# Six small changes in a two-layer hybrid decoder kernel: first products, one weight subtraction, the output projection's split, the index queries, the last selection rounds and the pins of late weights

## The chip, the cores and the metric

The kernel runs on one core of one Trainium2 chip. The metric is device time in microseconds (us), the median of several executions. The engines of the core are TensorE (PE: matrix products and transposes), VectorE (DVE: element-wise work and reductions), ScalarE (ACT: exponentials, casts, copies), GpSimd (POOL: some casts, subtractions and copies) and SyncE (SP), which issues most of the DMAs. Each engine runs its own list of instructions in the order of the program and waits on semaphores for the others.

## The reference

A sequence of 512 positions of width 1024 goes through two decoder layers, batch 1, all in float32. Layer 0 mixes by multi-head latent attention (MLA), layer 1 by a sparse attention (DSA). Each layer then attends with 4 heads to 256 memory tokens and ends with a gated feed-forward network. After every sub-layer comes `x <- LayerNorm(alpha * x + sublayer(x))`.

```
mla:  h = x @ w_in;  q = rms_norm(h[:, :512]) @ w_uq;  k, v = rms_norm(h[:, 512:768]) @ w_ukv  (+ rotary key, 32 wide)
      out = causal softmax(q k^T * 96^-0.5) v @ w_o                          # 16 heads, nope 64 + rope 32, v 64
dsa:  h = x @ w_in -> q (16 heads x 64), k, v (4 groups x 64), q_idx (8 x 64), k_idx (64), w_idx (8)
      index score = sum over 8 heads of  w_idx * relu(q_idx . k_idx / 8),  causal
      each query keeps its top 128 keys;  softmax(q k^T / 8 + rel_bias) v over those keys, then @ w_o
```

## The kernel before

The 512 positions are 4 query tiles of 128. A float32 factor is split into a high part (ACT casts it) and a low part (DVE or POOL subtracts the high part from the original, line L106), and each product is three matmuls: high by high, high by low, low by high (L137, L138, L139). Weights come by `chunk`: a DMA on SP into one of three `raw` buffers, a cast `wh` on ACT (L104), a subtraction `wl` on DVE or POOL (L106). `behind(ins)` asks that an instruction be put, on its own engine's list, after a given earlier point; the framework's scheduler then fixes the order of each list from its own estimates. So the order on an engine is not simply that of the source text.

**The start.** Eight small matmuls on an identity (`WARM`, L145) run before the data is there. Then the first projection of MLA takes the eight column blocks of `x` in order; for each block and tile it issues the three products together.

**The MLA middle.** The query part of the first projection is normalised tile by tile in `rms_t`: ACT sums the squares (L612), DVE and POOL make the reciprocal root (L298 on DVE, L300 on POOL), DVE scales (L615), PE transposes (L618), and ACT and DVE split the result. Two weights wait to be split there: `w_uk`, whose low part is a DVE instruction (L106 `wl<-raw,wh`, 128x1024) held behind the scaling of the last tile (`rms_scaled`), and the first of `w_uq`, whose low parts are POOL's. A raw buffer goes back to SP for the next weight when the low part of the old one has been made.

**The end of MLA.** `out_proj_parts` is a generator: it issues the products of the first piece `c == 0` of the output projection for the first half of the columns (24 matmuls), yields, and goes on after the last head's value products (`mla_pv(15)`).

**The DSA stage.** In the trace it lies between about 755 and 940 us. In order: the value and index-key projections; per pair of index heads `j` (0 to 3) a query projection, 12 score matmuls (L1130, L1131), 6 relus on ACT (L1133) and 6 accumulations on DVE (L1135, L1137); two key projections; eight query projections (`j` = 0 to 7); then attention over 16 items. An item is a query tile `qt` and a key group `g`, so item 4 is the first of tile 1 (keys 256 wide), item 8 the first of tile 2 (384 wide), item 12 the first of tile 3 (512 wide). Its steps are `s` (scores: PE L1205, L1206, L1207; bias add and minimum on DVE L498; exponential on ACT L505), `t` (transposes: PE L1220, split on ACT L104 and DVE L106) and `p` (values: PE L1251, L1252, L1262; ACT L1254; DVE L1259, L1263). Steps of the first items are run between the query projections (`steps`).

The top 128 keys of a query are found on DVE in 16 rounds for each of the tiles 1 to 3, 48 in all. A round is a maximum of 8 (L1149 `MAX8`) and a replacement of these 8 (L1150 `MATCH_REPLACE8`), 256, 384 or 512 wide. The rounds of a tile form one chain over one buffer. `NTK` says how many rounds stand in the source before each query projection, `NTI` how many after each later item; the scheduler may bring a round forward on DVE's list. When a tile's 16 rounds are done, ACT turns the buffer into a mask (L1156, `make_mask`), and PE adds that mask to the scores of that tile by a matmul (L1205).

**Queues around the output projection of DSA.** SP's list holds, in order, the reads of the relative bias for each item (L1186, `reads`), loads of the output weights `dsa_o` (L118) and reloads of the residual (L167). `pins` hold a weight load behind a certain bias read, and the POOL subtraction of the first weights behind a step of an item.

## Time and profile before

| | us |
|---|---|
| median of 3 executions (1501.17 to 1501.28) | 1501.27 |
| the profiled execution | 1501.13 |
| its span (first to last instruction) | 1499.3 |
| PE busy in the span | 1475.3 (98%) |
| DVE busy | 1041.7 (69%) |
| ACT busy | 672.8 (45%) |
| POOL busy | 401.6 (27%) |
| mean granted PE clock | 0.998 |

The span is the time from the first to the last instruction that the profile shows; 1.8 us of the profiled execution lie around it. A row of the timeline gives start, duration, engine, line, operation and the tiles by the program's names, then, in brackets, how long the engine had stood idle before it and what ended that. Rows of windows give for each engine its busy time and the count of instructions in a stretch, then the granted PE clock, the DMA share and the GB/s. Rows of groups give the count, the busy time and the mean duration of one. Line numbers in this document are those of the kernel before, unless a row of the order of the changed kernel is shown: there, lines from L582 on are 5 to 16 higher.

### The profile page before, as it was taken

The numbers are of one execution on the slowest core, as the hardware profiler recorded it, in microseconds if no ns is written. First come the engines' busy times: TensorE is split into PE (matmuls) and PEld (weight loads), VectorE is DVE, ScalarE is ACT, GpSimd is POOL, SyncE is SP. The second block draws the span as 40 slices with busy tenths as digits, with TensorE's granted clock in tenths as the row PEclk, the third lists the DMA queues.
The fourth block names the chain that finished last, engine by engine and source line by source line (L and its number), as shares of the span: only waits on it lengthen the run. The fifth ranks groups of instructions, "written<-read, shape, count | busy, mean of one in ns | idle before, by whom it ended". The sixth has DMA issues, their size and how long they took to land. (4 is left out here: it accounts for less than half of the span.)

```text
span 1499.3 us, 20324 instructions
## 1 busy us (share of the span) xinstructions
PE 1475.3 (98%) x7600; PEld 1258.1 (84%) x7600; DVE 1041.7 (69%) x1792; ACT 672.8 (45%) x1198; POOL 401.6 (27%) x368
## 2 busy tenths in 40 slices
PE   9999999999999999999999989999999999999998
PEld 8788888988888888888898768898889888888886
DVE  7766769667847656565778989685687575566656
ACT  4777743455233333333256688244542333334321
POOL 1454403010125223240025652030102233152302
PEclk9999999999999999999999999999999999999999
DMA  6244424423233332233333246353242333223231
GB/s 221 71 106 108 168 85 142 139 71 127 74 105 100 120 99 97 96 99 114 105 127 94 68 149 225 113 169 99 71 141 71 99 101 124 97 91 121 71 98 57
DMA packets 50282, 166.17 MB, mean 111 GB/s; under 512 B 5189, under 2 KB 11605, under 8 KB 47365
## 3 DMA queue, kind: packets, MB, share of 16 engines
q1 hardware_dynamic: 49460, 163.35, 33.6%
q10 hardware_dynamic: 720, 1.51, 0.3%
q8 instruction: 60, 0.98, 0.3%
q14 instruction: 42, 0.34, 0.1%
HBM read 160.60 MB, written 9.47 MB: 113 GB/s over the span
## 5 line engine op out<-in xcount | busy, mean ns | idle before, releaser
L137 PE MATMUL ps<-t,wh 128*128 128x512 f32 (+2 forms) x1184 | 433.3, 366 | 0.4 <-DVE t L106 0.3
L139 PE MATMUL ps<-t,wl 128*128 128x512 f32 (+2 forms) x1184 | 432.0, 365 | 1.4 <-DVE wl L106 1.4
L138 PE MATMUL ps<-t,wh 128*128 128x512 f32 (+2 forms) x1184 | 432.1, 365 | 0.0
L104 ACT CAST wh<-raw 128x1024 fp32r<-128x1024 f32 (+1 forms) x199 | 207.7, 1044 | 312.2 <-PE ps L138 136.5
L106 DVE TENSOR_TENSOR wl<-raw,wh 128x1024 fp32r<-128x1024 f32 (+2 forms) x170 | 234.8, 1384 | 108.9 <-ACT wh L104 108.0
L137 PE MATMUL ps<-wh,t 128*128 128x512 f32 (+2 forms) x736 | 281.7, 383 | 0.0
L138 PE MATMUL ps<-wl,t 128*128 128x512 f32 (+2 forms) x736 | 279.9, 380 | 0.1
L139 PE MATMUL ps<-wh,t 128*128 128x512 f32 (+2 forms) x736 | 279.5, 380 | 0.0
L139 PEld LDWEIGHTS ps<-t,wl 128*128 128x128 f32 x1184 | 223.3, 189 | 36.8 <-DVE wl L106 1.7
L137 PEld LDWEIGHTS ps<-t,wh 128*128 128x128 f32 x1184 | 223.3, 189 | 36.6 <-DVE t L106 1.6
L138 PEld LDWEIGHTS ps<-t,wh 128*128 128x128 f32 x1184 | 223.4, 189 | 34.5
L104 ACT CAST t<-ps 128x512 fp32r<-128x512 f32 (+3 forms) x241 | 118.2, 524 | 134.9 <-PE ps L368 85.9
L104 ACT CAST wh<-t 128x1024 fp32r<-128x1024 f32 (+1 forms) x84 | 82.3, 980 | 199.4 <-PE ps L138 163.8
L106 DVE TENSOR_TENSOR t<-ps,t 128x512 fp32r<-128x512 f32 (+3 forms) x241 | 137.8, 604 | 32.6 <-ACT t L104 31.4
L139 PEld LDWEIGHTS ps<-wh,t 128*128 128x128 f32 x736 | 138.5, 188 | 25.5
L137 PEld LDWEIGHTS ps<-wh,t 128*128 128x128 f32 x736 | 138.7, 188 | 24.9 <-ACT t L104 0.2
L138 PEld LDWEIGHTS ps<-wl,t 128*128 128x128 f32 x736 | 138.6, 188 | 24.9 <-DVE wl L106 0.5
L106 DVE TENSOR_TENSOR wl<-t,wh 128x1024 fp32r<-128x1024 f32 (+1 forms) x84 | 101.4, 1208 | 77.8 <-ACT wh L104 76.3
L300 POOL TENSOR_TENSOR sm<-sm,mhalf 128x1 f32<-128x1 f32 x32 | 28.3, 883 | 435.9 <-DVE sm L298 435.9
L104 ACT CAST t<-t 128x512 fp32r<-128x512 f32 (+3 forms) x133 | 75.4, 573 | 84.1 <-POOL t L944 51.6
L1015 DVE TENSOR_TENSOR t<-ps,t 128x512 f32<-128x512 f32 x44 | 30.4, 692 | 115.4 <-PE ps L139 115.4
L106 DVE TENSOR_TENSOR t<-t,t 128x512 fp32r<-128x512 f32 (+3 forms) x112 | 86.1, 775 | 33.1 <-ACT t L104 30.4
(184 smaller groups left out, 1924.8 us busy)
## 6 DMA issues: line engine op xcount, KB each, us to landing
raw<-in_ffn_in_dram SPq DMA_DIRECT2D x88, 512.0 KB, 3.5
t<-in_ffn_dg_dram SPq DMA_DIRECT2D x16, 1024.0 KB, 5.1
raw<-in_xa_k_dram SPq DMA_DIRECT2D x16, 512.0 KB, 3.6
raw<-in_xa_v_dram SPq DMA_DIRECT2D x16, 512.0 KB, 4.1
raw<-in_xa_q_dram SPq DMA_DIRECT2D x16, 512.0 KB, 3.6
scr<-vscr SPq DMA_DIRECT2D x16, 319.5 KB, 4.2
raw<-in_w_uq_dram SPq DMA_DIRECT2D x8, 512.0 KB, 3.9
raw<-in_mla_o_dram SPq DMA_DIRECT2D x8, 512.0 KB, 5.5
```

The costliest lines, as they stand in the source:

```text
L104: high[0] = nc.scalar.copy(h, src)
L106: low[0] = (eng or nc.vector).tensor_tensor(l, src, h.bitcast(F32), op=ALU.subtract)
L137: nc.tensor.matmul(ps, st[0], mv[0], start=start, stop=False, skip_group_check=more)
L138: nc.tensor.matmul(ps, st[0], mv[1], start=False, stop=False, skip_group_check=more)
L139: return nc.tensor.matmul(ps, st[1], mv[0], start=False, stop=stop, skip_group_check=more)
L300: power[0] = nc.gpsimd.tensor_tensor(b, a, mhalf, op=ALU.pow)
L1015: nc.vector.tensor_tensor(sg, pu, sg, op=ALU.mult)
```

## The change

- `WARM` is 9 instead of 8, and for the first column block the four tiles' high-by-high products come first, then the four high-by-low, then the four low-by-high.
- `rms_scaled` is taken before the five calls of `mla_v` and the last `rms_t`, so the low part of `w_uk` is held behind the scaling of the third tile, not of the fourth.
- `out_proj_parts` yields after piece `c == 1`, so 48 matmuls instead of 24 stand before the last head's value products. (The generator serves all output projections; only this call stops at the yield for other work.)
- The index queries of pair `j + 1` are projected before the scores of pair `j`.
- `NTK` ends with 2 instead of 4. Two rounds follow the last query projection and its steps, their maxima held behind `reduced[0]`, the latest bias add (L498) at that point, which is that of item 5. All later rounds of that tile chain behind them. The masks of tiles 2 and 3 are asked for one item earlier.
- The pins of `dsa_o` weights 3 to 7 are reads 10, 11, 12, 13, 14 in place of 6, 8, 10, 12, 14.

```
-WARM = 8
+WARM = 9
...
-                    if c == 0:
+                    if c == 1:
                         norm = yield
...
+            if k == 0:
+                for n, (x_, w_) in enumerate(((xh, wh), (xh, wl), (xl, wh))):
+                    for tt in range(NT):
+                        nc.tensor.matmul(ps2[tt][:, 0:NC0], x_[:, ts_of(tt)], w_, start=n == 0, stop=False)
+                continue
...
+    rms_scaled = scaled[0]
     for hv in range(5):
         mla_v(hv)
     rms_t(psq[NT - 1], 512, NT - 1, gq, cq)
     rms_end = high[0], low[0]
-    rms_power, rms_scaled = power[0], scaled[0]
+    rms_power = power[0]
...
+    waiting = index_queries(0)
+    for j in range(4):
+        ahead_q = index_queries(j + 1) if j < 3 else None
+        index_scores(j, waiting)
+        waiting = ahead_q
...
-    NTK, NTI = (5, 5, 5, 5, 5, 4, 4, 4), 2
+    NTK, NTI = (5, 5, 5, 5, 5, 4, 4, 2), 2
...
+    for _ in range(2):
+        topk(*todo.pop(0), reduced[0])
...
-        if n in (4, 8):
-            make_mask(2 + n // 8, outs[-1])
+        if n in (3, 7):
+            make_mask(2 + n // 7, outs[-1])
 
-    pins = [(reads[max(4, 2 * c)] if c > 2 else None, spreads[1 + 2 * c] if c < 5 else None) for c in range(NK)]
+    pins = [(reads[7 + c] if c > 2 else None, spreads[1 + 2 * c] if c < 5 else None) for c in range(NK)]
```

How the lists change is shown at three places. The first is DVE in the MLA middle (`wl` is the low part of `w_uk`, `t_113` the scaled last tile). Before:

```order
L298 TENSOR_SCALAR sm_596<-sm_594 128x1
L615 SCALAR_TENSOR_TENSOR t_113_600<-ps_485,sm_598,t_35_278 128x512
L106 TENSOR_TENSOR t_12_124<-ps_519,t_12_124 128x2x128
L106 TENSOR_TENSOR t_14_126<-ps_533,t_13_125 128x4x128
L106 TENSOR_TENSOR t_102_546<-ps_547,t_102_546 128x4x64
L106 TENSOR_TENSOR t_102_546<-ps_556,t_102_546 128x4x64
L106 TENSOR_TENSOR t_102_546<-ps_565,t_102_546 128x4x64
L106 TENSOR_TENSOR wl_632<-raw_629,wh_631 128x1024
```

and of the change:

```order
L298 TENSOR_SCALAR sm_597<-sm_595 128x1
L106 TENSOR_TENSOR wl_633<-raw_630,wh_632 128x1024
L106 TENSOR_TENSOR t_12_125<-ps_520,t_12_125 128x2x128
L106 TENSOR_TENSOR t_14_127<-ps_534,t_13_126 128x4x128
L106 TENSOR_TENSOR t_102_547<-ps_548,t_102_547 128x4x64
L106 TENSOR_TENSOR t_102_547<-ps_557,t_102_547 128x4x64
L106 TENSOR_TENSOR t_102_547<-ps_566,t_102_547 128x4x64
L620 SCALAR_TENSOR_TENSOR t_113_601<-ps_486,sm_599,t_35_279 128x512
```

The big subtraction moved from behind four or five low parts to the place right after the last tile's L298, and the scaling of the last tile moved behind those low parts.

The second place is ACT just after that (`t_13` from `ps_602` or `ps_603` is the high part of the last normalised tile, which the first query products read; `wh_929` or `wh_930` is the cast of the second `w_uq` weight, used by later heads). Before:

```order
L104 CAST t_13_125<-ps_602 128x4x128
L675 CAST t_115_609<-t_84_480 64x512
L676 CAST t_115_609<-t_84_480 64x512
L104 CAST t_115_609<-ps_635 64x512
L104 CAST wh_929<-raw_927 128x1024
```

and of the change:

```order
L104 CAST wh_930<-raw_928 128x1024
L104 CAST t_13_126<-ps_603 128x4x128
L681 CAST t_115_610<-t_84_481 64x512
L682 CAST t_115_610<-t_84_481 64x512
L104 CAST t_115_610<-ps_636 64x512 x2
```

The cast of the second `w_uq` weight now stands ahead of the cast that the first query products wait for. Likewise POOL's subtraction of that weight now stands ahead of its casts L681 and L682.

The third place is DVE around item 5's scores in the DSA stage (`t_1758` and `t_1756` are item 5, `t_1503` is the index score buffer of tile 3). Before, ahead of and at item 5:

```order
L1149 MAX m_1801_11774<-t_1503_10574 128x8
L1150 MATCH_REPLACE t_1503_10574<-m_1801_11774,t_1503_10574 128x512
L1149 MAX m_1802_11777<-t_1503_10574 128x8
L509 RECIPROCAL sm_11593<-sm_11500 128x4
L1150 MATCH_REPLACE t_1503_10574<-m_1802_11777,t_1503_10574 128x512
L1149 MAX m_1823_11848<-t_1503_10574 128x8
L1150 MATCH_REPLACE t_1503_10574<-m_1823_11848,t_1503_10574 128x512
L1149 MAX m_1824_11851<-t_1503_10574 128x8
L1259 TENSOR_TENSOR t_1748_11585<-ps_11580,t_1747_11583 64x256 x2
L498 ISA t_1758_11618,sm_11620<-ps_11622,t_1758_11618 128x256
```

and of the change, at and behind item 5:

```order
L498 ISA t_1756_11613,sm_11615<-ps_11635,t_1756_11613 128x256
L498 ISA sm_11615 128x1
L1165 MAX m_1763_11641<-t_1503_10575 128x8
L498 ISA t_1627_11135,sm_11647<-ps_11649,t_1627_11135 128x128
L498 ISA sm_11647 128x1
L106 TENSOR_TENSOR t_1752_11601<-ps_11595,t_1751_11600 128x512
L1166 MATCH_REPLACE t_1503_10575<-m_1763_11641,t_1503_10575 128x512
L106 TENSOR_TENSOR t_1755_11610<-ps_11604,t_1754_11609 128x512
L1165 MAX m_1764_11644<-t_1503_10575 128x8
L498 ISA t_1627_11135,sm_11647<-ps_11654,t_1627_11135 128x128
```

Before, the maxima of 15 of tile 3's 16 rounds stand ahead of item 5's first L498 and one round and a half stand between it and the first L498 of item 8. With the change 7 rounds stand ahead of it and 9 between item 5's last and item 8's first L498, each split by other work; nothing of tile 3's selection is left after item 8 begins in either.

## The prediction

> **What bounds the kernel now.** I read the page first: PE is busy for nearly the whole span, so time can be won only where PE stands still, and is lost wherever PE must wait anew.

> ```profile
> span 1499.3 us, 20324 instructions
> PE 1475.3 (98%) x7600; PEld 1258.1 (84%) x7600; DVE 1041.7 (69%) x1792; ACT 672.8 (45%) x1198; POOL 401.6 (27%) x368
> ```

> That leaves 24.0 us of PE idle time. The waits of PE say where it lies: of what the change touches, one wait in the MLA middle, and in the DSA stage (800 to 905 us) these:

> ```profile
> PE ps L1206 <- DVE sm L498: 2.6, 1, 2.6
> PE ps L1220 <- DVE t L1259: 1.3, 1, 1.3
> PE ps L1205 <- ACT t L1156: 0.7, 2, 0.5
> ```

> Columns are the total, the times and the longest. The timeline shows the first of these from both sides: PE finishes item 5's scores by 864.5, but the next score bank comes free only when DVE has done item 5's first L498, and that is queued behind selection rounds.

> ```profile
> 863.17 0.28 PE L1207 MATMUL ps<-t,t 128*128 128x256 f32 x1
> 864.23 0.28 PE L1207 MATMUL ps<-t,t 128*128 128x256 f32 x1
> 867.15 0.39 PE L1206 MATMUL ps<-t,t 128*128 128x256 f32 x1 [2.64 <-DVE sm L498]
> ...
> 863.67 0.69 DVE L1149 MAX8 m<-t 128x8 f32<-128x512 f32 x1
> 865.19 0.69 DVE L1149 MAX8 m<-t 128x8 f32<-128x512 f32 x1
> 866.66 0.42 DVE L498 CUSTOM_DVE_ANT_0 t<-ps,t 128x256 f32<-128x256 f32 x1
> 884.93 0.55 DVE L498 CUSTOM_DVE_ANT_0 t<-ps,t 128x384 f32<-128x384 f32 x1
> ```

> The last row is item 8's first L498. The windows (engine busy times in the order PE, PE loads, DVE, ACT, POOL) show a PE-bound stretch with a DVE that is nearly full, one where both wait for each other, and a rest where both have about 3 us free:

> ```profile
> 849.00:863.40 14.40, 14.40 (x80) 12.38 (x79) 14.01 (x43) 9.67 (x26) 8.53 (x13) 1.00 0.26 84
> 863.40:884.90 21.50, 16.83 (x100) 14.17 (x99) 18.29 (x63) 15.94 (x47) 12.41 (x20) 0.92 0.34 116
> 884.90:905.00 20.10, 17.20 (x101) 14.36 (x101) 16.96 (x54) 17.72 (x46) 11.25 (x22) 1.00 0.57 202
> ```

> The same windows for the two instructions of a round, L1149 and then L1150 (DVE busy, count):

> ```profile
> 849.00:863.40 14.40, 4.86 (x7) 1.00 0.26 84
> 863.40:884.90 21.50, 2.08 (x3) 0.92 0.34 116
> ```

> ```profile
> 849.00:863.40 14.40, 5.04 (x14) 1.00 0.26 84
> 863.40:884.90 21.50, 2.46 (x7) 0.92 0.34 116
> ```

> A 512-wide round costs (4.86 + 5.04) / 7 = 1.41 us of DVE. In the first window PE has no gap: there DVE does 9.9 us of rounds beside PE's query projections, for nothing.

> **The selection rounds, part by part.** The order shows that all rounds behind the 39th now come after item 5's last L498: the two held maxima carry the whole chain of tile 3 with them. So 9 rounds stand between item 5 and item 8, where 4.54 us of rounds lay.

> First, the wait removed. Item 5's first score is ready at 863.17 + 0.28 = 863.45, bound by PE in a window without gaps. DVE, relieved of its backlog, can take it at once instead of at 866.66. The 2.64 us wait goes.

> Second, what is late next. From item 5's first L498 to item 8's first L498 DVE has 18.29 - 4.54 = 13.75 us of other work, plus 9 x 1.41 = 12.7 us: 26.4 us, or about 25.5 if neighbouring rows, which overlap by some 0.1 us, are counted once. From 863.45 that ends at 889.0 to 889.9, against 884.93 before: 4.1 to 5.0 us later, and that only if DVE never waits. DVE's list is in order, so item 6's and 7's L498, L106 and L1259 stand behind these rounds, and PE's next score banks and transposes wait for them. I take 4.4. DVE meanwhile idles while PE projects the last queries: that cover is given up.

> Third, what PE catches up later. Item 8's transposes waited for ACT's cast and then DVE's L106:

> ```profile
> 888.68 0.69 DVE L106 TENSOR_TENSOR t<-ps,t 128x512 fp32r<-128x512 f32 x1 [0.43 <-ACT t L104]
> 898.87 0.63 PE L1220 MATMUL ps<-ident,t 128*128 128x128 f32 x4 [1.33 <-DVE t L1259]
> 902.45 0.50 PE L1205 MATMUL ps<-t,identb 128*128 128x512 f32 x1 [0.20 <-ACT t L1156]
> ```

> When DVE is the late one, the cast is ready sooner. DVE then has six L498 of items 8 and 9 ahead of that L106: from 884.93 + 4.4 = 889.3, at most 6 x 0.55 + 0.69 later is 893.3, against 889.37: 3.9 late or less, not 4.4. I count 3.7, a gain of 0.7. At 897.5 the new PE order has the first scores of item 12 where the 1.33 wait was (three 512-wide products, 0.7 us), and mask 3 is asked for earlier (0.2): 0.9. Net for the rounds: 4.4 - 0.7 - 0.9 = **+2.8 us**. Bounds: 4.1 less all of PE's idle time in the third window (20.1 - 17.2 = 2.9) is +1.2; 5.0 plus 0.8 for DVE's own waits on PE is +5.8.

> **The subtraction of w_uk.** These rows carry it:

> ```profile
> 46.17 0.15 DVE L298 TENSOR_SCALAR sm<-sm 128x1 f32<-128x1 f32 x1
> 50.09 2.66 DVE L106 TENSOR_TENSOR wl<-raw,wh 128x1024 fp32r<-128x1024 f32 x1
> ...
> L106 DVE TENSOR_TENSOR wl<-raw,wh 128x1024 fp32r<-128x1024 f32 x4 | 6.3, 1582 | 0.5 <-ACT wh L104 0.5
> ```

> ```profile
> 46.40 0.55 POOL L300 TENSOR_TENSOR sm<-sm,mhalf 128x1 f32<-128x1 f32 x1 [1.05 <-DVE sm L298]
> 46.92 4.74 POOL L106 TENSOR_TENSOR wl<-raw,wh 128x1024 fp32r<-128x1024 f32 x2
> ```

> ```profile
> 49.35 2.68 SPq L118 DMA_DIRECT2D raw<-in_w_uq_dram  x2
> ...
> raw<-in_w_uq_dram SPq DMA_DIRECT2D x3, 512.0 KB, 3.5
> ...
> 52.80 0.50 PE L139 MATMUL ps<-t,wl 128*128 128x512 f32 x1 [1.38 <-DVE wl L106]
> 53.83 0.85 PE L137 MATMUL ps<-t,wh 128*128 128x512 f32 x3
> ...
> 54.51 1.05 ACT L104 CAST wh<-raw 128x1024 fp32r<-128x1024 f32 x1
> 58.79 1.57 DVE L106 TENSOR_TENSOR t<-t,t 128x512 fp32r<-128x512 f32 x1 [0.69 <-ACT t L104]
> ```

> (A row of SP is a DMA's issue; 3.5 is its time to landing.) Before, the subtraction ran beside POOL's and took 2.66; the other three in that group took (6.33 - 2.66) / 3 = 1.22. PE waited 1.38 for it. Now it starts at 46.3, alone, and ends at 47.5: the 1.38 wait goes. But it runs against POOL's L300, which the last tile's scaling needs. L300 ends at 46.95 as before, or, if held, near 47.54 + 0.55 = 48.1. POOL's two subtractions, then the raw buffer's next load (before: issued at 49.35) move by 0 to 1.1, so that load lands at 52.9 to 54.0. ACT now has that load's cast (1.05) ahead of the cast of the last normalised tile (0.58): done at 54.5 to 55.6, with PE's first query product right behind, against 53.83: +0.7 to +1.8. Then POOL subtracts that weight (2.4) before L681 and L682, at the very time of DVE's L678; the 58.79 row, beside POOL's next subtraction, is 1.57 long for 0.69 of work, so up to 0.7 more is lost before the first scores. I take **+1.8**, nearer the held end because the 2.66 row shows these two engines holding each other. Bounds: -1.4 (only the wait goes) and +2.5.

> [...]

> **What I cost at nothing.**

> ```profile
> 10.43 0.41 PE L139 MATMUL ps<-wh,t 128*128 128x304 f32 x1
> PE ps L762 <- DVE t L106: 1.1, 1, 1.1
> 770.00:800.00 30.00, 29.93 (x161) 26.54 (x160) 18.31 (x35) 19.59 (x39) 12.72 (x7) 1.00 0.29 90
> 797.16 2.31 ACT L1133 ACTIVATE t<-ps 128x256 f32<-128x256 f32 x5 [0.27 <-PE ps L1131]
> 917.40 0.46 SPq L118 DMA_DIRECT2D raw<-in_dsa_o_dram  x1
> 922.70 0.40 PE L137 MATMUL ps<-wh,t 128*128 128x512 f32 x1
> ```

> First products: the one at 10.43 follows DVE's low part of the input by a few hundredths, so time won ahead of it is waited off there: 0, and -0.3 to +0.3. MLA's split point: around it PE's one wait is the L762 row, 1.1 at another head, and 24 matmuls, 0.23 us apart as in the 53.83 row ((0.85 - 0.40) / 2, a single one taking 0.40), 5.5 us in all, only change places: 0, at most 0.3 if the last head is late. Index queries: PE is busy 29.93 of 30 there, so nothing is to be won; twelve relus (0.46 each) for two score groups in a row could cost 0.5 if banks come free late. The last scores come some seven projection matmuls (1.6 us) earlier and the rounds with them, but PE has no wait on DVE from there to 864. Pins: the last weight was issued at 917.40 and would be 1 us or so later, while the first half's 96 products from 922.70 on take 22 us before it is used: 0. If that cover were gone, it would cost a landing.

> **Sum**, against the profiled execution's own 1501.13 (0.14 under the median): +1.8 + 2.8 + 0 = +4.6, that is 1505.7, or **1505.8 us** for the median.

> **Rivals.**

> *The subtraction only removes its wait* (L300 runs through and the load lands before ACT needs it), or PE catches up most of the rounds: 1501.3 - 1.4 + 2.8 = 1502.7, or 1501.3 + 1.2 + 0.7 = 1503.2. For it: 1.38 is a clear row. Against: the order on ACT. Chance 0.24, within 0.2%.

> *PE drops to half speed in the DVE-bound stretch.*

> ```profile
> 867.10:871.30 4.20, 4.02 (x19) 3.81 (x20) 3.94 (x20) 4.07 (x15) 2.81 (x6) 0.59 0.00 0
> ```

> After its 2.64 us wait PE was granted 0.59 of its clock for 4.2 us. In a 26 us stretch where PE has some 15 us of work (16.83 less the 1.7 below) this can come more than once; at 4.2 x 0.41 = 1.7 us each time, about once on the path, 1507.5. Chance 0.10. [...]

> *Faster: DVE is not the bound between items 5 and 8.* Then PE's 2.64, the 1.7 of half clock behind it, 0.7 for masks and 1.38 in MLA all go: 1501.3 - 6.4 = 1494.9; with the subtraction at +0.7, 1497.0. For it: DVE has 3.2 us idle in the second window and 3.1 in the third. Against: moved rounds are 12.7 - 4.5 = 8.2 us. The point that decides: item 8's first L498 by 884.9 (counted from unchanged work ahead). Chance 0.13.

> **How the numbers follow.** The forecast has 0.53, its own range 1503.4 (subtraction +0.7, rounds +1.4) to 1508.4 (+2.5 and +4.6). What a measurement can tell from no change is about 0.2%, 3.0 us: under 1498.3 is faster, over 1504.3 slower. Slower: nine tenths of the forecast and the half clock, 0.58. Within: the first rival and the rest of the forecast, 0.29. Faster: 0.13. The range reaches from 1498.5, near the third rival's edge, to 1508.8, four fifths of the way from the forecast to both upper bounds at once (1501.3 + 5.8 + 2.5 = 1509.6).

> **What would show it.** Right: no 2.64 wait at item 5; nine `MAX8` between items 5 and 8 with DVE over 95% busy, and 25 to 27 us between their first L498; PE waits there on L498, L106 and L1259 of 4 us or more in sum; no 1.38 wait for `wl` near 51, but one of 2 to 3 us for the cast of the last tile. Wrong: item 8's first L498 less than 23 us behind item 5's, L300 still 0.55 long beside the subtraction, or dsa_o products waiting for weights.

## The result, and the profile after

The changed kernel takes **1510.14 us** in the median (1509.54 to 1512.10), the kernel before 1501.28 beside it: a ratio of 1.0061, with a 95% interval of 1.0048 to 1.0074. It is slower, as predicted, but by 8.9 us and not by 4.5, and it lies above the predicted range, which ended at 1508.8.

The page of the changed kernel:

```profile
span 1508.0 us, 20333 instructions
...
PE 1480.0 (98%) x7602; PEld 1259.2 (84%) x7602; DVE 1040.7 (69%) x1792; ACT 672.5 (45%) x1198; POOL 404.2 (27%) x368
```

PE's idle time is 28.0 us, 4.0 more than before; the other 4.7 us of the longer span are PE at work, though the work is the same but for two of its 7602 products. So part of the loss is slower products: 1.7 of the 4.7 us lie in the MLA middle, where the granted clock falls (below). Another 3.4 lie in items 5 to 15, where both kernels have one stretch of half clock (3.41 us at 0.50, before from 867.77, after from 895.00); why they are there is not shown. (Line numbers from here on are those of the kernel that a row comes from: in the changed kernel L1221 is the old L1205, L1236 the old L1220, L1275 the old L1259, L1278 the old L1262.)

Where it arises is seen from the starts of one and the same PE instruction in both traces, here at the edges of the stages:

| place, start before | start after | later by | gained in between |
|---|---|---|---|
| 46.67, before the MLA middle | 47.03 | 0.36 | 0.36 (the start) |
| 74.11, behind the first heads | 77.61 | 3.50 | 3.14 (MLA middle) |
| 755.13, before the DSA stage | 758.72 | 3.59 | 0.09 |
| 858.20, before item 5's scores | 862.14 | 3.94 | 0.35 (index queries and first items) |
| 941.05, in the output projection | 949.66 | 8.62 | 4.68 (items 5 to 15) |
| 1480.07, near the end | 1488.71 | 8.64 | 0.02 |

The waits of PE in the changed kernel (total, times, longest):

```profile
PE ps L1221 <- DVE sm L498: 3.9, 5, 2.2
PE ps L137 <- ACT t L104: 3.0, 1, 3.0
PE ps L1236 <- DVE t L106: 1.9, 2, 1.3
...
PE ps L1139 <- ACT t L1142: 0.8, 3, 0.4
```

The 2.6 us at item 5 and the 1.4 us for `wl` are gone. In their place stand 2.2 us at item 8, more small waits on DVE, and 3.0 us for a cast of ACT. The timeline of the changed kernel shows the two places:

```profile
46.60 1.23 DVE L106 TENSOR_TENSOR wl<-raw,wh 128x1024 fp32r<-128x1024 f32 x1
...
46.76 1.48 POOL L300 TENSOR_TENSOR sm<-sm,mhalf 128x1 f32<-128x1 f32 x1 [1.04 <-DVE sm L298]
...
50.64 0.80 SPq L118 DMA_DIRECT2D raw<-in_w_uq_dram  x2
...
54.07 1.04 ACT L104 CAST wh<-raw 128x1024 fp32r<-128x1024 f32 x1 [2.56 <-DMA raw<-in_w_uq_dram]
55.02 0.58 ACT L104 CAST t<-ps 128x512 fp32r<-128x512 f32 x1
...
55.66 1.65 PE L137 MATMUL ps<-t,wh 128*128 128x512 f32 x3 [2.95 <-ACT t L104]
...
867.43 0.42 DVE L498 CUSTOM_DVE_ANT_0 t<-ps,t 128x256 f32<-128x256 f32 x1 [2.83 <-PE ps L1223]
...
893.75 0.55 DVE L498 CUSTOM_DVE_ANT_0 t<-ps,t 128x384 f32<-128x384 f32 x1
...
894.36 0.44 PE L1221 MATMUL ps<-t,identb 128*128 128x384 f32 x1 [2.16 <-DVE sm L498]
...
897.50 0.69 DVE L106 TENSOR_TENSOR t<-ps,t 128x512 fp32r<-128x512 f32 x1 [0.43 <-ACT t L104]
```

In the MLA middle ACT stands for 2.56 us before the cast of a weight that has not landed, and the cast of the last normalised tile, whose transposes PE (L623) had done by 52.0, is next in ACT's list. In the DSA stage item 5's and item 8's first L498 (867.43 and 893.75) lie 26.32 us apart, against 18.27 before (866.66 and 884.93). The windows say what fills that time, and show something that the waits do not (after the length come the busy times with their counts, first PE, then PEld, DVE, ACT and POOL, and at the end the granted clock, the DMA share and the GB/s):

```profile
55.66:58.90 3.24, 3.24 (x8) 2.59 (x9) 3.18 (x4) 1.66 (x3) 2.63 (x2) 0.53 0.27 85
...
867.43:893.75 26.32, 19.50 (x104) 13.18 (x102) 25.30 (x80) 15.38 (x45) 13.74 (x24) 1.00 0.30 94
...
895.00:898.40 3.40, 3.17 (x11) 2.69 (x11) 2.84 (x12) 3.38 (x11) 0.80 (x2) 0.50 0.19 78
...
896.00:912.00 16.00, 15.06 (x85) 12.61 (x84) 13.87 (x43) 15.85 (x41) 7.35 (x13) 0.92 0.37 121
```

DVE is 96% busy between the two items. Behind each of the two long waits PE is granted half its clock for about 3.4 us, which loses 1.7 us of its speed each time. And behind item 8 ACT is 99% busy for 16 us. The count of `MAX8` between the two items, in the changed kernel and then before (DVE busy, count):

```profile
867.43:893.75 26.32, 6.14 (x9) 1.00 0.30 94
```

```profile
866.66:884.93 18.27, 0.69 (x1) 0.91 0.27 86
```

### The profile page after: what moved, and what is told of

Its sections match the earlier page's. It is cut to its first block, busy times and chain, and to the rows that moved or that the text cites. A ratio compares the mean times of both kernels' runs of the same rounds, so it can differ in the third digit from the quotient of the medians.

```text
span 1508.0 us, 20333 instructions
## 1 busy us (share of the span) xinstructions
PE 1480.0 (98%) x7602; PEld 1259.2 (84%) x7602; DVE 1040.7 (69%) x1792; ACT 672.5 (45%) x1198; POOL 404.2 (27%) x368
## 4 chain that ended last, share of the span: by engine, by line
PE 86%; DVE 6%; ACT 3%; issue 2%; DMA 2%; POOL 1%; SPq 0%; DVEq 0%; ACTq 0%; POOLq 0%
PE ps L137 27%; PE ps L138 26%; PE ps L139 26%; DVE t L1166 1%; PE ps L368 1%; DVE m L1165 1%; PE ps L741 1%; DVE t L106 1%; ACT t L104 1%; DMA raw<-in_w_cq_dram 1%; PE ps L768 1%; ACT wh L104 1%; PE ps L1236 1%; PE ps L769 1%; ACT t L505 1%
## 5 line engine op out<-in xcount | busy, mean ns | idle before, releaser
L137 PE MATMUL ps<-t,wh 128*128 128x512 f32 (+2 forms) x1184 | 434.3, 367 | 3.4 <-ACT t L104 3.0
L139 PE MATMUL ps<-t,wl 128*128 128x512 f32 (+2 forms) x1184 | 432.1, 365 | 0.0
L104 ACT CAST wh<-raw 128x1024 fp32r<-128x1024 f32 (+1 forms) x199 | 207.9, 1045 | 323.3 <-PE ps L138 137.8
L106 DVE TENSOR_TENSOR wl<-raw,wh 128x1024 fp32r<-128x1024 f32 (+2 forms) x170 | 233.4, 1376 | 111.6 <-ACT wh L104 111.0
L137 PE MATMUL ps<-wh,t 128*128 128x512 f32 (+3 forms) x732 | 280.0, 383 | 0.0
L139 PE MATMUL ps<-wh,t 128*128 128x512 f32 (+3 forms) x732 | 278.2, 380 | 0.1
L138 PE MATMUL ps<-wl,t 128*128 128x512 f32 (+3 forms) x732 | 278.3, 380 | 0.0
L137 PEld LDWEIGHTS ps<-t,wh 128*128 128x128 f32 x1184 | 223.7, 189 | 40.3 <-ACT t L104 3.4
L139 PEld LDWEIGHTS ps<-t,wl 128*128 128x128 f32 x1184 | 223.4, 189 | 34.9
L104 ACT CAST t<-ps 128x512 fp32r<-128x512 f32 (+3 forms) x241 | 118.4, 524 | 136.2 <-PE ps L368 85.9
L104 ACT CAST wh<-t 128x1024 fp32r<-128x1024 f32 (+1 forms) x84 | 82.6, 983 | 199.8 <-PE ps L138 163.7
L106 DVE TENSOR_TENSOR t<-ps,t 128x512 fp32r<-128x512 f32 (+3 forms) x241 | 138.4, 605 | 35.9 <-ACT t L104 35.0
L139 PEld LDWEIGHTS ps<-wh,t 128*128 128x128 f32 x732 | 137.5, 188 | 25.8 <-DVE t L106 0.4
L137 PEld LDWEIGHTS ps<-wh,t 128*128 128x128 f32 x732 | 137.6, 188 | 24.6
L106 DVE TENSOR_TENSOR wl<-t,wh 128x1024 fp32r<-128x1024 f32 (+1 forms) x84 | 101.5, 1208 | 78.2 <-ACT wh L104 76.6
L300 POOL TENSOR_TENSOR sm<-sm,mhalf 128x1 f32<-128x1 f32 x32 | 29.3, 914 | 437.2 <-DVE sm L298 437.2
L104 ACT CAST t<-t 128x512 fp32r<-128x512 f32 (+3 forms) x133 | 75.6, 574 | 83.5 <-POOL t L950 51.7
L106 DVE TENSOR_TENSOR t<-t,t 128x512 fp32r<-128x512 f32 (+3 forms) x112 | 85.8, 772 | 33.3 <-ACT t L104 30.6
## 6 DMA issues: line engine op xcount, KB each, us to landing
raw<-in_ffn_in_dram SPq DMA_DIRECT2D x88, 512.0 KB, 3.5
raw<-in_xa_k_dram SPq DMA_DIRECT2D x16, 512.0 KB, 3.6
raw<-in_xa_v_dram SPq DMA_DIRECT2D x16, 512.0 KB, 4.3
raw<-in_xa_q_dram SPq DMA_DIRECT2D x16, 512.0 KB, 3.6
raw<-in_w_uq_dram SPq DMA_DIRECT2D x8, 512.0 KB, 4.4
raw<-in_mla_o_dram SPq DMA_DIRECT2D x8, 512.0 KB, 5.7
```

Of the source, the lines that this page charges most:

```text
L104: high[0] = nc.scalar.copy(h, src)
L106: low[0] = (eng or nc.vector).tensor_tensor(l, src, h.bitcast(F32), op=ALU.subtract)
L137: nc.tensor.matmul(ps, st[0], mv[0], start=start, stop=False, skip_group_check=more)
L138: nc.tensor.matmul(ps, st[0], mv[1], start=False, stop=False, skip_group_check=more)
L139: return nc.tensor.matmul(ps, st[1], mv[0], start=False, stop=stop, skip_group_check=more)
L300: power[0] = nc.gpsimd.tensor_tensor(b, a, mhalf, op=ALU.pow)
```

## The experiments

The first theory (A) follows the stages: the MLA part costs 3.1 us (some 1.4 of lateness and 1.7 of half clock), the rounds 4.7, the rest next to nothing. The rivals are given with each run. Under "MLA" and "DSA" stands how much later than before (negative: earlier) PE leaves these stretches than it enters them, read as in the table of stages above; the entry and exit of DSA here are 848 and 945 us of before. "5 to 8" is the time from item 5's to item 8's first L498.

| run | us | ratio to before, 95% | MLA | DSA | 5 to 8 |
|---|---|---|---|---|---|
| the change | 1510.14 | 1.0048 to 1.0074 | +3.14 | +4.66 | 26.32 |
| e1 no early subtraction | 1506.07 | 1.0021 to 1.0048 | 0.0 | +4.40 | 26.30 |
| e2 no moved rounds | 1506.58 | 1.0022 to 1.0044 | +4.75 | +1.10 | 17.94 |
| e3 neither | 1502.10 | 1.0002 to 1.0020 | 0.0 | 0.0 | 16.97 |
| e4 ACT's order mended | 1505.14 | 1.0018 to 1.0040 | -1.25 | +4.97 | 26.31 |
| e5 MLA wait filled | 1508.99 | 1.0033 to 1.0061 | +2.61 | +4.73 | 26.31 |
| e6 = e4, rounds as before | 1501.51 | 0.9990 to 1.0008 | -1.21 | +1.07 | 17.37 |
| e7 = e6, rounds spread | 1500.79 | 0.9987 to 1.0005 | -1.26 | +0.20 | 17.95 |
| e8 = e6, six rounds held | 1502.92 | 0.9999 to 1.0017 | -1.23 | +2.42 | 22.43 |
| e9 = e4, less ACT | 1505.65 | 1.0019 to 1.0040 | -1.23 | +5.03 | 26.31 |
| e10 = e7, less ACT | 1496.75 | 0.9960 to 0.9983 | -1.19 | -3.53 | 17.94 |
| e11 = e7, mask on POOL | 1497.09 | 0.9964 to 0.9984 | -1.20 | -3.11 | 17.91 |
| e12 = e4, mask on POOL | 1504.94 | 1.0015 to 1.0037 | -1.28 | +5.09 | 26.39 |
| e13 = e6, mask on POOL | 1499.62 | 0.9983 to 1.0001 | -1.19 | +0.94 | 18.57 |
| e14 = e12, waits filled | 1504.99 | 1.0014 to 1.0034 | -1.20 | +4.33 | 26.39 |

The kernel before was run again beside each group of runs. Its median was 1501.28 us beside the change and e5 to e8, 1500.82 beside e1 to e4, 1501.12 beside e9 to e11, 1501.01 beside e12 and e13, and 1501.32 beside e14. So rows of different groups can lie 0.5 us apart for that reason alone; where it matters, the distance of each run from its own kernel before is used below.

**e1 to e3: which part costs what.** One part, the other, and both put back.

```
e1:  rms_scaled = scaled[0] again behind the last rms_t
e2:  NTK back to (..., 4); no held rounds; masks at n in (4, 8)
e3:  both
```

> The changed kernel with only the early subtraction of w_uk undone (it is again ordered behind the scaling of the last normalised tile). Theory A (the trace of the changed kernel read stretch by stretch: PE is 0.4 us late when the MLA middle begins and 3.5 us late when it ends, so this part costs 3.1): 1510.1 - 3.1 = 1507.0 us, PE's wait for the cast of the last tile (2.95 us at 52.7) gone, the wait for wl (1.4) back, and the granted clock at 1.00 between 55 and 59 us. Rival B (the sizes on record hold, +1.8 for this part, and the rest of the loss lies in the parts costed at nothing): 1508.3 us. Rival C (the two parts hide each other's loss): no change, 1510.1 us.

> The changed kernel with only the selection rounds and the two later masks put back as before (four rounds ahead of the last query projection, none held behind item 5's scores, masks asked for at the old iterations). Theory A (PE is 3.9 us late when the DSA stage begins and 8.6 us late when it ends, so the rounds cost 4.7): 1510.1 - 4.7 = 1505.4 us, the 2.6 us wait at item 5's scores back, the 2.2 us wait at item 8's gone. Rival B (the record's +2.8): 1507.3 us.

> The changed kernel with both parts undone; what is left are the order of the first products, MLA's split point, the index queries one group ahead and the pins of the last weights. Theory A (shifts outside the two parts: 0.1 at the start, 0.3 near 34 us, 0.05 in MLA, 0.3 in the index stage): 1501.3 to 1502.1 us, within 0.1% of before. Rival B (the loss that the record did not foresee lies in these parts, some 4 us): 1505 us.

Without the early subtraction the kernel is 4.1 us faster, without the rounds 3.6, without both 8.0 (3.6, 3.1 and 7.6, each counted from its own kernel before). So the four other edits together are worth little (e3 is 1.0011 times before, its interval just above 1), rival B falls, and rival C too. e2 came out above its forecast, and its MLA part is worse than in the changed kernel though nothing there differs. Its window says why:

```profile
54.20:61.10 6.90, 5.72 (x14) 4.52 (x15) 4.54 (x5) 3.42 (x6) 4.95 (x3) 0.53 0.45 156
```

Here the half clock lasted 6.8 us and lost 3.4 us of speed, not 1.7, and the MLA part cost 4.75, not 3.14. Its DSA stage, too, lost 1.10 us in this trace. Its executions range from 1503.95 us at a mean granted clock of 0.997 to 1507.81 at 0.994. Less the lost clock, the lateness is the same in both: 3.14 - 1.71 = 1.43 and 4.75 - 3.41 = 1.34.

**e4: ACT's order or POOL's hold.** Both were in the prediction's chain; this run mends the first and leaves the second.

```
chunk(A["w_uq"][pr], ...):  for pr == 2 the cast wh<-raw is ordered behind the last tile's cast (rms_end[0])
```

> The changed kernel with one more ordering: the cast of the third w_uq load stands on ACT behind the cast of the last normalised tile, as it did before; the subtraction of w_uk stays early. Theory A (ACT stands in order before a cast whose load has not landed, and the tile's cast, ready near 52.2, waits behind it to 55.0; the 2.95 us wait then drops PE's clock for 3.2 us): the wait goes, the clock stays at 1.00, the MLA part ends 3 to 4.5 us earlier: 1505.6 to 1507.1 us. Rival D (what makes PE late is the hold of POOL's rsqrt power behind the subtraction, not ACT's order): the tile's scaling comes as late as before, 1509 to 1510 us.

5.0 us faster than the changed kernel, or 4.5 counted from the kernels before: at the upper end of the 3 to 4.5 expected, or above it. The timeline of e4:

```profile
46.38 1.48 POOL L300 TENSOR_TENSOR sm<-sm,mhalf 128x1 f32<-128x1 f32 x1 [1.05 <-DVE sm L298]
...
51.66 0.59 ACT L104 CAST t<-ps 128x512 fp32r<-128x512 f32 x1 [0.53 <-PE ps L623]
...
52.30 0.96 PE L137 MATMUL ps<-t,wh 128*128 128x512 f32 x3
...
53.91 1.05 ACT L104 CAST wh<-raw 128x1024 fp32r<-128x1024 f32 x1
```

POOL's L300 is held exactly as long (1.48), the tile's cast runs at 51.66 in place of 55.02, PE does not wait for it, and the clock does not drop there. So the early subtraction itself gains 1.25 us, about the 1.38 wait that it removes; what cost 3.1 was a cast that moved ahead of another on ACT's list as a by-product. Rival D falls.

**e5: is it the wait or the clock?**

```
+ for _ in range(12 if h == 0 else 0):
+     nc.tensor.matmul(pq, wk[0][:, 0, 0:P], ckv[0][:, 0], start=True, stop=True)
  # pq is then started anew by the first query product
```

> The changed kernel with twelve products added that no result uses: they repeat w_uk's first product into the bank of the first query product, which then starts that bank anew, so that TensorE works through most of its 2.95 us wait for the cast of the last tile. Theory A (the wait itself costs 1.43 us of lateness, and the idle time drops the granted clock to 0.5 for one or two stretches of 3.4 us, 1.7 us each): the clock stays at 1.00 from 55 to 62 us and the time falls by 1.7 us, to 1508.4 (1508.1 to 1508.8). Rival E (the clock drops for another reason, or the half-speed matmuls are waited off at the first scores): 1510.1, no change.

1.15 us faster: between the two forecasts, nearer theory A than rival E. The windows of e5 and the wait that takes its place:

```profile
52.00:55.50 3.50, 3.23 (x15) 2.31 (x13) 0.00 (x0) 1.54 (x3) 1.20 (x2) 1.00 1.03 386
55.54:62.00 6.46, 6.01 (x24) 4.42 (x24) 5.23 (x6) 2.70 (x5) 4.52 (x3) 1.00 0.30 107
```

```profile
62.22 0.39 PE L137 MATMUL ps<-t,t 128*128 128x256 f32 x1 [0.45 <-ACT t L104]
```

With PE kept busy the clock stays at 1.00: the idle time was its cause. But the faster PE then waits 0.45 at the first scores. So between 0.5 us (the stretch in this trace) and 1.6 (e2 against the changed kernel, one more piece of 1.7) of each piece of half clock lands on the path in this place.

**e6: the early subtraction alone.** e4 and the rounds of before.

> The changed kernel with ACT's order as in the fourth experiment and the selection rounds and masks as before: the early subtraction alone, without its side effect. Theory A (the MLA part then ends 1.2 to 1.4 us earlier than in the kernel before, as that trace shows, and the other parts are worth nothing): 1.3 us under the third experiment, 1500.8 us; no wait of 1 us or more between 46 and 58 us. Rival F (what is won in the MLA middle is given back at the DSA stage): 1502.1, as the third experiment.

1501.51, between the two forecasts and not to be told from the kernel before. In the trace the MLA part gains its 1.21 us, and the DSA stage loses 1.07: its 2.6 us wait at item 5 is followed by half clock, where e3 with a wait as long (2.61) had none (the last section shows how the two waits lie). The windows of e6 and then of e3, behind that wait:

```profile
866.66:870.00 3.34, 3.34 (x17) 3.21 (x18) 3.08 (x15) 3.24 (x11) 2.58 (x5) 0.56 0.00 0
```

```profile
867.42:873.00 5.58, 5.45 (x39) 4.88 (x40) 4.99 (x27) 5.48 (x20) 3.02 (x6) 1.00 0.06 10
```

This does not explain the difference by itself (before had the drop too, and no loss against e3). But the traced execution was the slowest of e6's eleven, 0.8 us above the median, and counted from the kernels before e6 lies 1.0 us under e3 (+0.23 against +1.28), near the 1.3 of theory A. Whether a part of the gain is given back, the scatter of the two runs does not tell.

**e7 and e8: how many rounds stand between two items.**

```
e7:  later rounds per item {3: 2, 4: 2, 5: 1, 6: 1, 7: 1}; the last four held: two behind item 5's L498, one behind item 8's, one behind item 9's
e8:  the last six rounds held behind item 5's L498
```

> As the sixth experiment, but the last four selection rounds are held back singly: one each behind item 5's scores, behind the next items and behind items 8 and 9, so that one round stands between two items and not several ahead of one. Theory G (before item 8 what costs is the number of rounds that stand in one place of DVE's list; DVE has some 3 us free in each of the two stretches behind item 5): the 2.6 us wait at item 5's scores goes, none of 1.5 us or more takes its place, and the time falls by 1 to 2.5 us from the sixth: 1498.5 to 1500. Rival H (DVE is the bound over the whole stretch from 863 to 905 us, so that the wait only moves): 1500.8, no change.

> As the sixth experiment, but the last six rounds are held behind item 5's scores, so that about six rounds stand between item 5 and item 8, where the fourth experiment has nine and the sixth two. Theory A (DVE does 13.75 us of other work there and 1.41 us for each round, and item 8's scores wait for all of it): item 8's first L498 comes 26.3 - 3 x 1.41 = 22.1 us behind item 5's, and the time is 1505.1 - 4.2 = 1500.9 us. Rival I (the hold and the earlier masks cost, not the number of rounds): 1505 us, as the fourth.

The two ends of the stretch in e8:

```profile
862.81 0.42 DVE L498 CUSTOM_DVE_ANT_0 t<-ps,t 128x256 f32<-128x256 f32 x1 [2.61 <-PE ps L1224]
...
885.24 0.55 DVE L498 CUSTOM_DVE_ANT_0 t<-ps,t 128x384 f32<-128x384 f32 x1
```

Six rounds give 22.43 us, as forecast (22.1), and nine 26.3: some 1.3 us for each round, close to its 1.41 us of DVE time. The time, 1502.9, fell by 2.2 us from e4 (2.7 counted from the kernels before), neither by 4.2 nor by nothing: item 8 came 1.0 us later than before, counted from the entry of the stage, yet the stage ended 2.4 later, with 3.4 us of speed lost to half clock in it. e7 shows the same from the other side: item 8 comes 3.5 us earlier than before, and nothing of it is left at the end. Its time, 1500.79, cannot be told from before (rival H).

**e9 to e11: what holds the stretch behind item 8.** In the changed kernel ACT is 99% busy there, so the runs take work off it. e9 and e10 leave casts out (see their text). e11 moves the masks to POOL, and with that it also drops their hold: `make_mask` had put each of the last two behind the latest value copy (`outs[-1]`) on ACT's list.

```
e9, e10:  for qt == 2, g > 0, kb < 2:  Ph = item 8's Ph; only Pl is made
e11:  nc.gpsimd.tensor_scalar(mk, masks[qt], -1e38, 4.0, op0=is_gt, op1=mult)   in place of ACT's Relu held behind outs[-1]; held behind nothing
```

> The fourth experiment (all rounds moved, ACT's cast order mended) with ACT relieved behind item 8: items 9, 10 and 11 do not cast the first two of their three transposed blocks but use item 8's in their place (so their outputs are computed from other numbers), which takes six ACT casts of about 0.5 us out of that stretch; DVE's subtractions and PE's products stay. Theory J (what was 4.9 us late at item 8's first L498 is never caught up because ACT is then full, 99% busy for 16 us, and sets the pace until the last weights): 2 to 3 us less than the fourth, 1502.1 to 1503.1 us. Rival K (DVE or PE sets the pace there, or the half-speed clock): under 0.7 us less, 1504.4 to 1505.1.

> The seventh experiment (rounds spread one by one) with the same six ACT casts left out as in the ninth (items 9 to 11 again use item 8's blocks). Theory J (the seventh was 5.5 us ahead of before at 891 us and gave it back because ACT was full): 2 to 3 us less than the seventh, 1497.8 to 1498.8 us. Rival K (PE's own work bounds that stretch): 1500.3 or more.

> The seventh experiment with the masks of tiles 1 to 3 made on POOL, by one comparison and product, where ACT made them; the kernel computes the same. Theory J: about 0.7 us of ACT work leaves the full stretch: 1500.0 to 1500.5 us. Rival L (POOL makes the mask later than ACT did, and the first scores of items 8 and 12 wait for it): 1501 to 1502 us.

With the rounds spread, both gain far more than expected: 4.0 and 3.7 us from e7 (3.9 and 3.5 counted from the kernels before). e11 leaves nothing out and is **1497.09 us, 0.9974 of the kernel before (0.9964 to 0.9984)**: faster than both kernels. The timeline shows the last round and the mask of tile 3, first in e7 (with two other rows of ACT), then in e11:

```profile
889.58 0.68 DVE L1167 MATCH_REPLACE8 t<-m,t 128x512 f32<-128x512 f32 x1
...
894.10 1.05 ACT L104 CAST wh<-raw 128x1024 fp32r<-128x1024 f32 x1 [1.25 <-DMA raw<-in_dsa_o_dram]
...
899.76 0.58 ACT L1271 COPY t<-ps 64x512 f32<-64x512 f32 x1
900.25 0.72 ACT L1173 ACTIVATE t<-t,four 128x512 fp32r<-128x512 f32 x1
```

```profile
889.48 0.67 DVE L1167 MATCH_REPLACE8 t<-m,t 128x512 f32<-128x512 f32 x1
...
891.76 1.93 POOL L1172 TENSOR_SCALAR t<-t 128x512 fp32r<-128x512 f32 x1
```

The rounds are done by 890.3 in both. On ACT the mask starts at 900.25, directly behind the value copy that the source holds it behind. That ACT is full, as theory J had it, does not explain this: ACT stood idle for 1.25 us before 894.10, time enough for the mask's 0.72. POOL, 2.7 times as slow at it but free of the hold, has it by 893.7. So e11 changes two things, the engine and the hold. A mask on ACT without the hold was not run, and how much of the gain belongs to which is not shown, here and in e12 to e14. The window behind that, of e7 and then of e11:

```profile
896.60:904.00 7.40, 5.12 (x20) 3.83 (x21) 5.70 (x14) 6.61 (x16) 3.96 (x6) 0.77 0.51 198
```

```profile
896.30:904.00 7.70, 6.83 (x38) 4.89 (x37) 6.69 (x18) 7.17 (x18) 4.21 (x7) 1.00 0.59 212
```

In e11 PE has item 12's first scores to fill its waits with from 896 on, and with the waits the half clock behind them goes: 0.77 against 1.00 in this window, 1.7 us. With the rounds in one block (e9) the same casts win nothing: J falls for the changed kernel. But there PE ran at half clock, as two overlapping windows of e9 show:

```profile
892.00:908.00 16.00, 14.69 (x81) 12.73 (x80) 12.57 (x36) 13.42 (x32) 7.47 (x12) 0.89 0.34 115
888.00:896.00 8.00, 6.70 (x25) 6.41 (x26) 7.28 (x25) 6.64 (x20) 0.82 (x3) 0.57 0.34 134
```

ACT is at 84% and no longer full, and PE loses 3.4 us of speed. So e9 does not tell whether one cover had only taken the other's place.

**e12 to e14: the block of rounds again.** e12 and e13 move the masks in e4 and in e6, again without the hold; e14 fills the two waits ahead of item 8 in e12:

```
e14:  + if (qt, g) == (2, 0):  14 matmuls of 128x512 into a spare bank
```

> The fourth experiment (all rounds moved, ACT's cast order mended) with the masks made on POOL as in the eleventh. Theory M (behind item 8 the mask of tile 3 waits its turn on a full ACT, 10 to 12 us behind the last round, and PE has nothing to fill its waits with until then; this holds with the rounds moved in one block too): 2 to 4 us less than the fourth, 1501.1 to 1503.1 us, with item 8's first L498 still 26.3 us behind item 5's. Rival N (with the rounds in one block the time is lost ahead of item 8 and no mask can win it back): within 0.7 us of the fourth, 1504.4 to 1505.8.

> The sixth experiment (early subtraction, ACT's cast order mended, rounds as before) with the masks made on POOL: the mask's engine alone, without the spread rounds. Theory M: the waits behind item 8 shrink, 1 to 2 us less than the sixth, 1499.5 to 1500.5 us, and the spread rounds of the eleventh are worth the rest to 1497.1. Rival O (the mask alone does it): 1497.1 as the eleventh. Rival P (the mask is worth nothing while item 8 comes as late as before): 1501.5.

> The twelfth experiment (rounds in one block, masks on POOL, ACT's cast order mended) with fourteen products that no result uses, into a bank of their own, ahead of the last transposes before item 8: 14 x 0.23 = 3.2 us of work in place of the 1.3 and 2.2 us waits there. Theory A (PE's idle time drops its clock to 0.5 for 3.4 us just where it has to make up for item 8's lateness, 1.7 us): the clock stays at 1.00 from 885 to 897 us, item 8's first L498 is no later, and the time falls by 1.2 to 1.7 us from 1504.9, to 1503.2 to 1503.7. Rival Q (the half-speed products are waited off elsewhere, at DVE): 1504.7 to 1505.2.

e12 stays where e4 was (rival N), e13 gains 1.9 us over e6 (1.6 counted from the kernels before; the intervals of the two ratios overlap). That is theory M's size, though its reason, a full ACT, is not shown. So of e11's gain over e6, 4.4, the mask is worth some 1.9 and the spread 2.5 if they are taken in this order; the spread alone, e7 against e6, gave 0.7, inside the scatter. e14 changes nothing (rival Q). The window of e14 around item 8:

```profile
884.77:897.00 12.23, 11.42 (x65) 9.88 (x66) 11.22 (x35) 7.35 (x22) 4.10 (x7) 1.00 0.30 107
```

Item 8's first L498 and the waits of PE behind it, from the timeline of e14:

```profile
889.21 0.55 DVE L498 CUSTOM_DVE_ANT_0 t<-ps,t 128x384 f32<-128x384 f32 x1
...
896.32 0.63 PE L1240 MATMUL ps<-ident,t 128*128 128x128 f32 x4 [0.81 <-DVE t L1279]
...
902.43 0.50 PE L1225 MATMUL ps<-t,identb 128*128 128x512 f32 x1 [1.17 <-DVE sm L498]
```

The clock is full, PE, no longer slow, waits for DVE instead, and the stage still ends 4.33 us later. So in the DSA stage the half clock was not what cost. What is left is item 8's lateness, 4.9 us in this trace.

## Why the prediction was wrong in size

The direction and both mechanisms were right; two terms of the sum were mis-sized. (The sum itself is 0.1 low: 4.6 us over the median of 1501.27 is 1505.9. Nothing hangs on it.)

**The MLA middle, taken as +1.8, was +3.14.** What it said of each link up to the first query product came true: the wait for `wl` went, L300 was held (1.48 us long for 0.55), the next weight's load moved back with POOL's subtractions, ACT's list had its cast ahead of the tile's, and the tile's cast was done at 55.6. The first query product came at 55.66 against 53.83, of which 0.36 had come from the start: 1.47 later, inside the 0.7 to 1.8. The step that failed is the next one, a term that the sum put at nothing here: what a wait of 2.95 us does to PE's clock. The text had the half clock as a rival, from a row of before, but only for the DSA stage and at 0.10. In the MLA middle it lost 1.71 us of speed, of which 0.5 to 1.6 reached the path (e5 and e2). And the sum took the lateness as the price of moving the subtraction early, whereas e4 shows that the move gains 1.25 and the order of two casts loses 4.4.

**The rounds, taken as +2.8, were +4.68.** Nine `MAX8` between items 5 and 8, DVE 96% busy, 26.3 us between the two L498: as it said (nine, over 95%, 25 to 27). Against the stage's own entry item 8 came 893.75 - 884.93 - 3.94 = 4.88 later: in the 4.1 to 5.0, 0.5 above the 4.4 taken. The step that failed is "what PE catches up later": 0.7 at item 8's transposes and 0.9 at the mask were credited, and 4.88 - 4.68 = 0.2 came. The first credit rested on DVE's free time ahead of an L106. But from item 8's first L498 to that L106 it is 3.75 us before (884.93 to 888.68) and 3.75 after (893.75 to 897.50): a chain from DVE to ACT, PE, ACT and back, as long whoever is late. The second was 0.2 for the mask of tile 3, asked for earlier, and 0.7 for item 12's first scores, which need that mask, in the place of a wait of PE. These are the rows of the mask, before and in the changed kernel, and there of these scores:

```profile
901.68 0.72 ACT L1156 ACTIVATE t<-t,four 128x512 fp32r<-128x512 f32 x1
```

```profile
905.81 0.72 ACT L1172 ACTIVATE t<-t,four 128x512 fp32r<-128x512 f32 x1
...
907.03 0.47 PE L1221 MATMUL ps<-t,identb 128*128 128x512 f32 x1 [0.59 <-DVE sm L498]
```

Less the 3.94 of the stage's entry, the mask came at 901.87, no earlier than before, and the scores at 903.09, later than the 902.45 before. The 0.7 also took PE's waits for free time to win back. They were not: with ACT's casts lightened (e9), the mask made elsewhere (e12) or the clock kept up (e14), PE waits for another engine and the total stays. Each was taken away singly or in a pair; a run without all three was not made, so which of them binds last stays open.

**The terms at nothing.** The start was +0.36, of which 0.27 is one wait at 34 us that ran from 0.41 to 1.06 us in kernels with the same order there: scatter. MLA's split point cost 0.09. The index queries and the first items cost 0.35, inside the "at most 0.5". No dsa_o product waited for its weights. e3 puts these edits at 0.3 us in its trace, and at 0.3 to 3 by the interval of its ratio.

**The rivals.** That PE would catch up most of the rounds, or the subtraction only remove its wait, did not come. "Faster" hung on item 8's first L498 by 884.9 counted from unchanged work ahead; it came at 893.75 - 3.94 = 889.8. The range's upper end was built from waits alone, and no bound held the clock in the MLA middle. With the half clock in the MLA term (4.2 x 0.41 = 1.7 by the row quoted there) and no catch-up, its own rows would have given 1501.3 + 1.8 + 1.7 + 4.4 = 1509.2, and the upper bounds would have held the result.

## What to carry to other kernels

When an edit moves one instruction early, read the lists of every engine for what changed places behind it, and ask of each cast whether its load has landed: in the changed kernel ACT stood for 2.56 us before one whose load had not, with work that was ready behind it. Count PE's waits together: in these traces the 14 pieces of 3.41 us in which they left PE busy for less than half (the last section counts them) were each followed by half clock, which lost 1.71 or 3.41 us of speed, and of 1.71 us lost in the MLA middle 0.5 to 1.6 reached the path. And do not credit time to be won back in a stretch where DVE, ACT and PE hand work around a ring (0.2 of the 1.6 us credited here came). What helped there was to put the queued rounds one piece between two steps and to make the mask as soon as its rounds were done (on POOL and without its hold, 1.93 us for ACT's 0.72, and still 1.6 to 1.9 us off the whole). And before putting a late instruction down to a full engine, read what the source holds it behind.

## What the runs showed of the hardware that was not expected

What goes with a fall in these traces is not the length of one wait but how long PE was busy in one piece of this grid. The traces hold 6946 pieces at full clock. In 14 of them PE was busy for less than half of the time, and behind all 14 the clock fell. Of 15 pieces at 52 to 61% it fell behind two (e1 and e4, where no single wait was longer than 1.27 us), and behind a busier one never. The 2.64 us wait of before, which lies in one piece (PE busy 19% of it), was followed by half clock, and the 2.61 us wait of e3, which an edge of the grid cuts in two (58% and 62%), was not. PE's busy time is the first number behind the length; first the piece of before, then the two of e3:

```profile
864.36:867.77 3.41, 0.65 (x4) 0.30 (x2) 3.30 (x12) 0.60 (x2) 3.35 (x3) 1.00 0.49 190
```

```profile
862.84:866.26 3.42, 1.97 (x18) 1.76 (x15) 3.32 (x9) 1.48 (x3) 2.87 (x3) 1.00 0.59 181
866.26:869.67 3.41, 2.13 (x16) 1.92 (x16) 3.19 (x16) 2.18 (x7) 3.33 (x5) 1.00 0.01 2
```

Why some falls last two pieces, and what sets the length of a piece, is not shown.
